# First token rows of an encoder layer: products of the identity on TensorE while they load, three row buffers of their own, and gate weights asked for behind the second and the fourth block

## The chip, the cores and the metric

The kernel runs on one core of one Trainium2 chip. The metric is the time of one execution in device microseconds (us), lower is better. The kernel before was timed three times: 1777.31, 1779.03 and 1780.24 us, median 1779.03.

## The reference

One layer of a streaming encoder, for 1024 prompt tokens and 64 sample tokens that share the weights (D = 1024, all float32):

```
h = rmsnorm(x, g_mix);  p = h @ w_in
qa, ka, va, qi, ki, wi, ub, qm, gates = split(p)
A: s = relu(qi . ki) per index head; score = sum_h s * wi; per query the top 256 (sample: 48)
   admissible keys by score; softmax attention over those
B: per channel group of 128: trailing mean over 2/4/8/16 frames minus the token, then a 128x128 map
M: cross-attention into 256 memory tokens
x = x + (sum over A, B, M of sigmoid(gate) * (branch @ w_o)) @ w_out
x = x + (silu(rmsnorm(x) @ w_gate) * (rmsnorm(x) @ w_up)) @ w_down
```

Keys, values and indexer keys of the new tokens are outputs too.

## The kernel before

The tokens lie in nine blocks of 128 rows, b = 0 to 8 (the last one, the sample, has 64). All of it runs on one core, each engine working through its own list of instructions in order. A scheduler writes those lists at build time: it plays the program through with durations of its own and appends, on each engine, what it believes ready first. So a change at the beginning can move instructions much later on. In-order lists make one instruction that waits hold up all that stand behind it on the same engine. Every DMA is issued from SyncE (SP), whose list is in order too.

Float32 products are made in three passes: each operand is split into a rounded part and a rest (`whi`/`wlo` for weights, `hh`/`hl` for the normalized, transposed tokens), and `matmul3` (L115 to L121, the products on L120) issues hi*hi, hi*lo and lo*hi.

The stages that the prediction speaks of, in program order:

- **First rows** (L242 to L259). For each block: load the rows (L247), square and sum them on ScalarE (L252), take the reciprocal root on GpSimd (L124, L125), scale them on VectorE (L255), transpose them on TensorE in eight 128x128 pieces into two PSUM tiles `mm` (L131), round each of these to `hh` on ScalarE (L133) and take the rest `hl` on VectorE (L86). Even blocks load into `raw`, the three general weight buffers, odd blocks into two buffers `xt`. Behind blocks 0 and 2 `fgate` asks for a block of gate weights: load to `fraw` (L110), round to `whi` on GpSimd (L96), rest `wlo` on VectorE (L86).
- **Gates** (`fsig`, L230; products `fl<-hh` and `fl<-hl` on L120). One gate block over all tokens is three chunks of 364, 362 and 362 columns with 24 products each. 16 gate blocks, 1152 products, are filler: they stand between the other stages wherever the scheduler had TensorE free.
- **Index stage** (L266 to L351). Index weights come through the `raw` buffers into `tmhi`/`tmlo` (`tm_weights`, L169, L96, L86; three pieces of 888, 888 and 592 columns); `idx_proj` makes 24 products of 296 columns per block; then scores of every query with every key (L333, L334, L338). Cached keys `ck` enter through L286 and L278/L279.
- **Search** (`select`, from L735). The top 256 are found by bisection over 31 bits on score tiles, for three blocks with ScalarE counting (L765, results compared by `hit_a`, L784) and four with VectorE counting (L768, `hit_v`). Both loops step together in VectorE's list.
- **Mixer** (branch B, L385 to L448), four channel groups one behind the other. Per group: 72 products, running sums on GpSimd (L431), then on VectorE `pw` (L433, L435, L434), ScalarE rounds it to `ph` (L440), VectorE takes the rest `pl`, and TensorE multiplies both by `pwh`, `pwl`. Then `fill_ob` (products `fl<-bh`) needs all four groups.
- Then query and key projections, attention, output projection, feed-forward.

```
for b in range(NB):
    t0, n = TS[b]
    xt = xp.tile([128, D], F32, name="xt", tag="xt", bufs=2) if b % 2 else raw_tile()
    SP.dma_start(xt[:n], xrows(b))
    ...
    A.activation(junk[:n], xt[:n], AF.Square, accum_out=ss[:n])
    rstd(r[:n], ss[:n], 1.0 / D)
    V.scalar_tensor_tensor(xt[:n], xt[:n], r[:n], gmix[:n], op0=OP.mult, op1=OP.mult)
    transpose_split(xt, n, hh[:, :, t0:t0 + n], hl[:, :, t0:t0 + n])
    if b in (0, 2):
        first.append(fgate(8 + len(first)))
```

Of the kernel before, what the change touches and what calls it, by code (L numbers as in the profile page):

```python
# [8 lines left out]
F32 = mybir.dt.float32  # L9
# [7 lines left out]
D = 1024  # L17
# [28 lines left out]
def encoder_step(ctx: ExitStack, tc: tile.TileContext, a: dict, o: list):  # L46
    nc = tc.nc
    V, A, G, PE, SP = nc.vector, nc.scalar, nc.gpsimd, nc.tensor, nc.sync
# [12 lines left out]
    ident_r = const.tile([128, 128], F32R, name="ident_r")  # L61
# [6 lines left out]
    def bcast_row(dst, src, off, n):  # L68
        SP.dma_start(dst, bass.AP(tensor=src.tensor, offset=src.offset + off, ap=[[0, 128], [1, n]]))
# [7 lines left out]
    def mm(dt=F32):  # L77
        return psum[0].tile([128, 512], dt, name="mm", tag="mm", bufs=n_mm[0])
# [44 lines left out]
    def rstd(r, ss, inv):  # L123
        G.tensor_scalar(r, ss, inv, EPS, op0=OP.mult, op1=OP.add)  # L124
        G.tensor_tensor(r, r, mhalf[:r.shape[0], :r.shape[1]], op=OP.pow)  # L125

    def transpose_split(src, n, hi, lo):
        for g in range(0, KT, 4):
            ps = mm()
            for k in range(4):  # L130
                PE.transpose(ps[:, k * 128:k * 128 + n], src[:n, (g + k) * 128:(g + k + 1) * 128], ident[:n, :n])  # L131
            pv = ps.rearrange("p (k t) -> p k t", t=128)[:, :, :n]
            A.copy(hi[:, g:g + 4], pv)  # L133
            lo_of(lo[:, g:g + 4], pv, hi[:, g:g + 4])
# [59 lines left out]
    def xrows(b):  # L194
        return a["x_prompt"][b * 128:(b + 1) * 128] if b < 8 else a["x_sample"]

    def raw_tile():
        return wp.tile([128, 1024], F32, name="raw", tag="raw", bufs=3)
# [26 lines left out]
    def fgate(f):  # L225
        return wblock(a["w_gates"][f], (KT, 128), fraw())
# [14 lines left out]
    ip = ip_c.__enter__()  # L241
    with tc.tile_pool(name="xphase", bufs=1) as xp:  # L242
        gmix = xp.tile([128, D], F32, name="gmix")
        for b in range(NB):
            t0, n = TS[b]
            xt = xp.tile([128, D], F32, name="xt", tag="xt", bufs=2) if b % 2 else raw_tile()
            SP.dma_start(xt[:n], xrows(b))  # L247
            if b == 0:
                bcast_row(gmix, a["g_mix"], 0, D)
            junk = xp.tile([128, D], F16, name="xjunk", tag="xjunk", bufs=1)  # L250
            ss = xp.tile([128, 1], F32, name="ss", tag="ss", bufs=3)
            A.activation(junk[:n], xt[:n], AF.Square, accum_out=ss[:n])  # L252
            r = xp.tile([128, 1], F32, name="rs", tag="rs", bufs=3)
            rstd(r[:n], ss[:n], 1.0 / D)
            V.scalar_tensor_tensor(xt[:n], xt[:n], r[:n], gmix[:n], op0=OP.mult, op1=OP.mult)  # L255
            transpose_split(xt, n, hh[:, :, t0:t0 + n], hl[:, :, t0:t0 + n])
            if b in (0, 2):
                first.append(fgate(8 + len(first)))

    gqm_c = col("gqm_c", a["g_qm"], 1)  # L260
# [92 lines left out]
    with tc.tile_pool(name="mem", bufs=1) as mp:  # L353
# [6 lines left out]
        for i in range(2):  # L360
            xt = raw_tile()
# [88 lines left out]
    with tc.tile_pool(name="qm", bufs=1) as tp:  # L450
        for half in range(2):
            w = tm_weights(tp, a["w_qm"][half], 256)
            for b in range(NB):
                t0, n = TS[b]
# [6 lines left out]
    with tc.tile_pool(name="qa", bufs=1) as qp:  # L461
# [18 lines left out]
        for half in range(2):  # L480
            w = tm_weights(qp, a["w_qa"][half], 256)
            for b in range(NB):
                t0, n = TS[b]
# [28 lines left out]
        for b in range(NB):  # L512
            t0, n = TS[b]
# [822 lines left out]
```

## Time and profile before

| | |
|---|---|
| median of three runs | 1779.03 us (1777.31 to 1780.24) |
| the profiled execution's own time | 1782.27 us |
| its span, first to last instruction | 1780.5 us |
| TensorE products busy | 1721.8 us (97% of the span), 11810 instructions |
| VectorE busy | 1127.0 us (63%) |
| ScalarE busy | 816.4 us (46%) |
| GpSimd busy | 403.3 us (23%) |
| mean granted TensorE clock | 0.991 |

Engines: PE is TensorE, DVE VectorE, ACT ScalarE, POOL GpSimd, SPq the DMA issues of SyncE. L12 is line 12 of the kernel. The granted clock is a share of full speed: 1.00 is 2.4 GHz, 0.50 is 1.2 GHz. Products overlap in the pipeline: what one costs in a run of them is the distance between two starts, not its own duration.

### The profile page before, as it was taken

To read this page: it belongs to the slowest core of one execution; us is meant where nothing else is said; L and a number is where in the kernel's file an instruction comes from. 1 tells how busy PE (TensorE), PEld (TensorE's weight loads), DVE (VectorE), ACT (ScalarE), POOL (GpSimd) and SP (SyncE) were. 2 spreads that over 40 slices of the span, in tenths; PEclk is the share of its full clock that TensorE was granted. 3 is DMA by queue.
4 is the path that set the end of the run, shared out by engine and by line. 5 is a ranking of instruction groups with operands and counts; after the bars stand their busy time and mean duration, and the time that the engine had idled before them with its cause. 6 is when DMAs were issued, how large, how long until landed. Compare 5 with 4: busy or idle time off the path is not lost.

```text
span 1780.5 us, 31511 instructions
## 1 busy us (share of the span) xinstructions
PE 1721.8 (97%) x11810; PEld 1672.4 (94%) x11810; DVE 1127.0 (63%) x2411; ACT 816.4 (46%) x1927; POOL 403.3 (23%) x444
## 2 busy tenths in 40 slices
PE   7999999999999998989899998999999999999999
PEld 6999999989999998877798997999999999999999
DVE  6567999998953345779783858645444444544443
ACT  5456677726523443579631444433333333433332
POOL 4111423343531223765203521100000000000000
PEclk9999999999999999999999998999999999999999
DMA  7122541134355236640454333222222221857562
GB/s 230 60 67 76 164 141 57 58 98 137 118 157 176 84 97 233 188 154 1 165 184 146 98 120 110 92 73 73 73 73 77 92 75 38 316 184 239 187 229 98
DMA packets 128582, 224.26 MB, mean 126 GB/s; under 512 B 23463, under 2 KB 86303, under 8 KB 128430
## 3 DMA queue, kind: packets, MB, share of 16 engines
q1 hardware_dynamic: 128430, 222.26, 38.5%
q8 instruction: 93, 1.52, 0.3%
q14 instruction: 59, 0.48, 0.1%
HBM read 167.84 MB, written 54.37 MB: 125 GB/s over the span
## 4 chain that ended last, share of the span: by engine, by line
PE 61%; DVE 6%; DMA 2%; issue 1%; POOL 1%; ACT 1%; SPq 0%; DVEq 0%; ACTq 0%; POOLq 0%
PE mm L1115 24%; PE mm L1263 14%; PE mm L120 11%; PE fl L120 7%; PE acc L921 1%; PE tr L891 1%; DVE lo L86 1%; PE mm L914 1%; DVE wlo L86 1%; DVE fr L1071 1%; DMA side_a<-gt 1%; DVE ws L1078 0%; PE mm L603 0%; DVE pr L895 0%; DVE pl L86 0%
## 5 line engine op out<-in xcount | busy, mean ns | idle before, releaser
L1115 PE MATMUL mm<-hi,whi 128*128 128x288 f32 (+1 forms) x1120 | 324.0, 289 | 9.4 <-ACT whi L1107 8.3
L1115 PE MATMUL mm<-hi,wlo 128*128 128x288 f32 (+1 forms) x1120 | 324.9, 291 | 0.0
L1115 PE MATMUL mm<-lo,whi 128*128 128x288 f32 (+1 forms) x1120 | 324.2, 290 | 0.0
L1115 PEld LDWEIGHTS mm<-hi,whi 128*128 128x128 f32 x1120 | 212.6, 190 | 10.1 <-ACT whi L1107 8.5
L1115 PEld LDWEIGHTS mm<-lo,whi 128*128 128x128 f32 x1120 | 212.5, 190 | 0.0
L1115 PEld LDWEIGHTS mm<-hi,wlo 128*128 128x128 f32 x1120 | 211.9, 189 | 0.2 <-DVE wlo L86 0.2
L120 PE MATMUL fl<-hl,whi 128*128 128x362 f32 (+1 forms) x576 | 190.5, 331 | 0.0
L120 PE MATMUL fl<-hh,whi 128*128 128x362 f32 (+1 forms) x576 | 189.9, 330 | 0.6 <-ACT hh L133 0.6
L120 PE MATMUL fl<-hh,wlo 128*128 128x362 f32 (+1 forms) x576 | 189.3, 329 | 0.0
L1263 PE MATMUL mm<-uh,wh 128*128 128x362 f32 (+1 forms) x512 | 167.4, 328 | 0.0
L1263 PE MATMUL mm<-ul,wh 128*128 128x362 f32 (+1 forms) x512 | 166.8, 326 | 0.0
L1263 PE MATMUL mm<-uh,wl 128*128 128x362 f32 (+1 forms) x512 | 166.0, 326 | 0.0
L86 DVE TENSOR_TENSOR wl<-raw,wh 128x1024 fp32r<-128x1024 f32 x64 | 78.4, 1225 | 126.1 <-ACT wh L94 125.8
L94 ACT CAST wh<-raw 128x1024 fp32r<-128x1024 f32 x64 | 67.3, 1051 | 148.9 <-PE mm L1263 137.5
L120 PE MATMUL mm<-tmhi,hh 128*128 128x256 f32 (+3 forms) x432 | 122.8, 289 | 0.5 <-POOL tmhi L96 0.5
L120 PE MATMUL mm<-tmlo,hh 128*128 128x256 f32 (+3 forms) x432 | 122.5, 286 | 0.3 <-DVE tmlo L86 0.3
L120 PE MATMUL mm<-tmhi,hl 128*128 128x256 f32 (+3 forms) x432 | 122.3, 285 | 0.0
L765 ACT ACTIVATE junk_a<-score,cand_a,sgn_a 128x512 f16<-128x512 f32 (+2 forms) x93 | 95.5, 1027 | 46.8 <-DVE cand_a L782 22.7
L86 DVE TENSOR_TENSOR wlo<-raw,whi 128x1024 fp32r<-128x1024 f32 (+1 forms) x75 | 76.1, 1027 | 55.0 <-ACT whi L1107 39.7
L120 PEld LDWEIGHTS fl<-hh,whi 128*128 128x128 f32 x576 | 108.3, 188 | 1.6 <-issue 1.0
L120 PEld LDWEIGHTS fl<-hl,whi 128*128 128x128 f32 x576 | 108.4, 188 | 0.6
L120 PEld LDWEIGHTS fl<-hh,wlo 128*128 128x128 f32 x576 | 108.5, 188 | 0.6
(386 smaller groups left out, 4538.5 us busy)
## 6 DMA issues: line engine op xcount, KB each, us to landing
raw<-in_w_down_dram SPq DMA_DIRECT2D x66, 512.0 KB, 3.7
raw<-in_w_up_dram SPq DMA_DIRECT2D x26, 512.0 KB, 3.7
fraw<-in_w_gates_dram SPq DMA_DIRECT2D x24, 512.0 KB, 4.0
fr<-in_w_gate_dram SPq DMA_DIRECT2D x22, 512.0 KB, 3.6
side<-side_a SPq DMA_DIRECT2D x8, 1088.0 KB, 6.0
raw<-in_w_out_dram SPq DMA_DIRECT2D x16, 512.0 KB, 3.7
uf<-u SPq DMA_DIRECT2D x44, 181.0 KB, 3.7
u<-tg SPq DMA_DIRECT2D x22, 288.0 KB, 2.1
```

The source lines that it names most:

```text
L86: V.tensor_tensor(lo, src, hi.bitcast(F32), op=OP.subtract)
L94: A.copy(hi, src)
L120: PE.matmul(ps, l, r, start=i == 0, stop=i == n - 1)
L765: A.activation(junk[:n, :nk], sc, AF.Sign, bias=bj, scale=1.0 if scale is None else scale[:n, j:j + 1], accum_out=sj)
L891: PE.matmul(lg[:n, i * 512:i * 512 + cn], qT[:, h, :n], kT[:, kv, s, k0 + c:k0 + c + cn], start=s == 0, stop=s == 1)
L914: PE.transpose(pt[:cn, i * n:(i + 1) * n], probs[i][:, c:c + cn], ident[:n, :n])
L921: PE.matmul(acc, vv, r, start=ji == 0 and i == 0, stop=ji == nj - 1 and i == 1)
L1071: V.scalar_tensor_tensor(hb[e][:, :n], ys[i][:, kk], gffn_c[:, kk:kk + 1], rb[:, :n], op0=OP.mult, op1=OP.mult)
L1115: PE.matmul(dst[i], l, r, start=start and j == 0, stop=stop and j == 11, skip_group_check=True)
L1263: PE.matmul(acc[f], l, r, start=kb == 0 and j == 0, stop=kb == NF - 1 and j == 2)
```

## The change

Three edits in the loop over the first rows, and nothing elsewhere:

1. Before the loop 40 products of the 128x128 identity with itself are issued, and 20 more behind each of the blocks 0 and 1. They write a PSUM tile `spin` out of the five `mm` buffers that nobody reads. They need only `ident_r`, which is made on the core.
2. All blocks load into `xt`, which has three buffers now, and none into `raw`.
3. Gate weights are asked for behind blocks 1 and 3 rather than 0 and 2.

```
+        spin = mm()
+
+
+        def turn_over(n):
+            for _ in range(n):
+                PE.matmul(spin[:, :128], ident_r, ident_r, start=True, stop=True)
+
+        turn_over(40)
         for b in range(NB):
             t0, n = TS[b]
-            xt = xp.tile([128, D], F32, name="xt", tag="xt", bufs=2) if b % 2 else raw_tile()
+            xt = xp.tile([128, D], F32, name="xt", tag="xt", bufs=3)
             SP.dma_start(xt[:n], xrows(b))
...
             transpose_split(xt, n, hh[:, :, t0:t0 + n], hl[:, :, t0:t0 + n])
-            if b in (0, 2):
+            if b < 2:
+                turn_over(20)
+            if b in (1, 3):
                 first.append(fgate(8 + len(first)))
```

Lines behind the edit are 8 to 10 higher in the changed kernel (L255 becomes L263, L433 becomes L443).

SyncE's list. Before, five blocks of rows can be asked for at once: rows 0, `gmix`, gate weights, rows 1, 2, 3, 4, then the small `gqm_c`, `gffn_c`, `spool_c`, `cosi`, `sini`, `gk`, `ck`, then rows 6, gate weights, rows 5, 8, 7, then the index weights. Now: rows 0, `gmix`, rows 1, gate weights, rows 2, the same small ones up to `gk`, then the three pieces of index weights, `ck`, gate weights, rows 3, two blocks of memory rows, rows 4, a block of memory weights, gate weights, rows 5 and 6; rows 7 and 8 stand behind the first stores of gate results. Rows 3 can be asked for when the transposes of block 0 have freed their buffer.

VectorE's list at its head, before, from the scaling of block 0 on (`raw` and `xt` are rows):

```order
L255 SCALAR_TENSOR_TENSOR raw<-raw,rs,gmix 128x1024
L86 TENSOR_TENSOR wlo<-fraw,whi 128x1024
L86 TENSOR_TENSOR hl<-mm,hh 128x4x128
L255 SCALAR_TENSOR_TENSOR xt<-xt,rs,gmix 128x1024
L86 TENSOR_TENSOR hl<-mm,hh 128x4x128
L255 SCALAR_TENSOR_TENSOR raw<-raw,rs,gmix 128x1024
L263 TENSOR_SCALAR spool_c<-spool_c 128x4
L255 SCALAR_TENSOR_TENSOR xt<-xt,rs,gmix 128x1024
L86 TENSOR_TENSOR hl<-mm,hh 128x4x128
L255 SCALAR_TENSOR_TENSOR raw<-raw,rs,gmix 128x1024
L86 TENSOR_TENSOR hl<-mm,hh 128x4x128
L279 TENSOR_TENSOR k_364<-ck,k_364 128x64
```

And now, from the same place:

```order
L263 SCALAR_TENSOR_TENSOR xt<-xt,rs,gmix 128x1024 x2
L86 TENSOR_TENSOR wlo<-fraw,whi 128x1024
L273 TENSOR_SCALAR spool_c<-spool_c 128x4
L263 SCALAR_TENSOR_TENSOR xt<-xt,rs,gmix 128x1024
L86 TENSOR_TENSOR tmlo<-raw,tmhi 128x888
L86 TENSOR_TENSOR hl<-mm,hh 128x4x128 x2
L86 TENSOR_TENSOR tmlo<-raw,tmhi 128x888
L289 TENSOR_TENSOR k_445<-ck,k_445 128x64
L86 TENSOR_TENSOR tmlo<-raw,tmhi 128x592
L86 TENSOR_TENSOR wlo<-fraw,whi 128x1024
L86 TENSOR_TENSOR hl<-mm,hh 128x4x128 x2
L263 SCALAR_TENSOR_TENSOR xt<-xt,rs,gmix 128x1024
```

The rests `hl` of block 0 stand now behind a piece of the index weights (`tmlo`), those of block 1 behind the rest of these, the cached keys and the second gate weights; those of block 2 follow only behind the scaling of block 3. On TensorE the transposes of block 3 likewise stand ahead of the run of products of the first chunk, which needs blocks 0 to 2; before, those of blocks 3 and 4 did.

TensorE's list around the first product of the index stage (`mm_370`), before, with the buffers' numbers; `fl_4292` is a gate block on the second chunk of columns, and the transposes are those of block 8:

```order
L131 MATMUL mm_319<-ident_69,raw_310 128x64 x4
L131 MATMUL mm_326<-ident_69,raw_310 128x64 x4
L282 MATMUL mm_367<-ident_r_74,k4_364 128x128
L120 MATMUL fl_4292<-hl_105,whi_138 128x362
L120 MATMUL fl_4292<-hh_104,wlo_139 128x362
L120 MATMUL fl_4292<-hh_104,whi_138 128x362
L120 MATMUL mm_370<-tmhi_347,hh_104 128x296
```

And now (the index stage begins with `mm_451`; `fl_4401` is the second chunk, `fl_4429` and `fl_4457` are the third):

```order
L131 MATMUL mm_400<-ident_69,xt_391 128x64 x4
L131 MATMUL mm_407<-ident_69,xt_391 128x64 x4
L292 MATMUL mm_448<-ident_r_74,k4_445 128x128
L120 MATMUL fl_4401<-hh_104,whi_294 128x362
L120 MATMUL fl_4401<-hl_105,whi_294 128x362
L120 MATMUL fl_4401<-hh_104,wlo_295 128x362
L120 MATMUL fl_4401<-hh_104,whi_294 128x362
L120 MATMUL fl_4401<-hl_105,whi_294 128x362
L120 MATMUL fl_4401<-hh_104,wlo_295 128x362
L120 MATMUL fl_4429<-hh_104,whi_242 128x362
L120 MATMUL fl_4457<-hh_104,whi_294 128x362
L120 MATMUL mm_451<-tmhi_428,hh_104 128x296
```

More of the filler stands ahead of the index stage: before its first product 98 gate products instead of 72, before its last score product 584 instead of 551. At the first `ph` product of the fourth mixer group both lists have the same products behind them, all 1152 gate products and the first 27 of `fill_ob` among them (the change has its 80 products of the identity besides).

VectorE's list at the fourth mixer group, before (`hit_a` compares a step of the search):

```order
L771 TENSOR_SCALAR score_95<-score_95,sgn_a 128x512
L768 TENSOR_SCALAR junk_v,ssum_v<-score_96,cand_v 128x640
L433 TENSOR_TENSOR pw<-pw,fix 128x16
L435 SCALAR_TENSOR_TENSOR pw<-pw,e 128x1087
L771 TENSOR_SCALAR score_97<-score_97,sgn_a 128x768
L768 TENSOR_SCALAR junk_v,ssum_v<-score_98,cand_v 128x896
L434 TENSOR_TENSOR pw<-pw,e 128x16
L784 TENSOR_TENSOR hit_a<-ssum_a,cuta_a 128x3
```

And now:

```order
L794 TENSOR_TENSOR hit_a<-ssum_a,cuta_a 128x3
L781 TENSOR_SCALAR score_99<-score_99,sgn_a 128x1024
L794 TENSOR_TENSOR hit_v<-ssum_v,cuta_v 128x4
L795 SCALAR_TENSOR_TENSOR tbit_a<-hit_a,tbit_a 128x3
L795 SCALAR_TENSOR_TENSOR tbit_v<-hit_v,tbit_v 128x4
L798 TENSOR_SCALAR tbit_a<-tbit_a 128x3
L792 TENSOR_SCALAR cand_v<-tbit_v 128x4
L799 TENSOR_SCALAR cand_a<-tbit_a 128x3
L803 TENSOR_SCALAR shi_a<-tbit_a 128x3
L778 TENSOR_SCALAR junk_v,ssum_v<-score_100,cand_v 64x192
L800 TENSOR_SCALAR cand_a<-cand_a 128x3
L443 TENSOR_TENSOR pw<-pw,fix 128x16
```

The fourth group's `pw` stands behind 31 steps of the search now, all there are; before it stood behind 30. From the key attention on (L861) the lists of all engines are the same.

## Rows read from the trace of the kernel before

**Rows 1.** Busy time by stretch, all engines (stretch, length, busy us of each, PEclk, DMA, GB/s)
```profile
0.00:40.00 40.00, 27.10 (x156) 24.88 (x157) 29.98 (x72) 21.56 (x41) 18.61 (x30) 1.00 0.74 229
172.00:352.00 180.00, 177.86 (x1133) 176.19 (x1132) 171.31 (x488) 127.17 (x266) 59.84 (x47) 1.00 0.34 106
```
**Rows 2.** Timeline of TensorE, first 35 us (start, us, line, out<-in, count, idle before)
```profile
7.90 1.97 PE L131 MATMUL mm<-ident,raw 128*128 128x128 f32 x8 [7.90 <-DVE raw L255]
...
21.30 0.64 PE L120 MATMUL fl<-hl,whi 128*128 128x364 f32 x1
...
29.11 0.33 PE L120 MATMUL fl<-hl,whi 128*128 128x364 f32 x1
29.28 0.33 PE L120 MATMUL fl<-hh,wlo 128*128 128x364 f32 x1
29.44 1.04 PE L131 MATMUL mm<-ident,xt 128*128 128x128 f32 x8
...
33.57 0.66 PE L131 MATMUL mm<-ident,xt 128*128 128x128 f32 x4 [1.45 <-DVE hl L86]
```
**Rows 3.** Timeline of the fourth mixer group, on VectorE and TensorE
```profile
352.67 0.17 DVE L433 TENSOR_TENSOR pw<-pw,fix 128x16 f32<-128x16 f32 x1
...
357.64 0.76 PE L120 MATMUL mm<-ph,pwh 128*128 128x364 f32 x3 [1.09 <-ACT ph L440]
...
359.99 0.67 PE L120 MATMUL mm<-pl,pwh 128*128 128x364 f32 x1 [1.59 <-DVE pl L86]
```
**Rows 4.** Timeline of SyncE: three issues of the first 15 us
```profile
2.58 0.73 SPq L247 DMA_DIRECT2D raw<-in_x_prompt_dram  x1
...
3.84 0.45 SPq L247 DMA_DIRECT2D raw<-in_x_prompt_dram  x1
...
14.02 0.43 SPq L286 DMA_DIRECT2D ck<-in_cache_idx_k_dram  x1
```
**Rows 5.** The same three issues in the DMA view (count, KB, us from issue to landing)
```profile
raw<-in_x_prompt_dram SPq DMA_DIRECT2D x1, 512.0 KB, 7.7
...
raw<-in_x_prompt_dram SPq DMA_DIRECT2D x1, 512.0 KB, 9.4
...
ck<-in_cache_idx_k_dram SPq DMA_DIRECT2D x1, 16.0 KB, 3.5
```
**Rows 6.** Timeline of the other engines, first 36 us
```profile
2.27 0.22 DVE L62 CAST ident_r<-ident 128x128 fp32r<-128x128 f32 x1
...
4.45 1.06 ACT L252 ACTIVATE xjunk<-raw 128x1024 f16<-128x1024 f32 x1 [2.45 <-DMA raw<-in_x_prompt_dram]
...
6.56 1.28 DVE L255 SCALAR_TENSOR_TENSOR raw<-raw,rs,gmix 128x1024 f32<-128x1024 f32 x1 [3.77 <-POOL rs L125]
...
21.68 1.21 DVE L86 TENSOR_TENSOR wlo<-fraw,whi 128x1024 fp32r<-128x1024 f32 x1
...
26.20 0.93 POOL L96 TENSOR_SCALAR tmhi<-raw 128x888 fp32r<-128x888 f32 x1
...
28.13 1.07 DVE L86 TENSOR_TENSOR tmlo<-raw,tmhi 128x888 fp32r<-128x888 f32 x1
...
32.84 3.06 DVE L86 TENSOR_TENSOR hl<-mm,hh 128x512 fp32r<-128x512 f32 x5
```
**Rows 7.** Two stretches at the low clock (stretch, length, TensorE busy, PEclk, DMA, GB/s)
```profile
360.00:366.40 6.40, 6.40 (x20) 0.50 0.20 77
1086.00:1090.00 4.00, 4.00 (x15) 0.50 0.00 0
```
**Rows 8.** Timeline of VectorE: two comparisons of the search, one step apart
```profile
333.24 0.16 DVE L784 TENSOR_TENSOR hit_a<-ssum_a,cuta_a 128x3 int32<-128x3 f32 x1 [0.41 <-ACT junk_a L765]
...
337.37 0.16 DVE L784 TENSOR_TENSOR hit_a<-ssum_a,cuta_a 128x3 int32<-128x3 f32 x1 [0.27 <-ACT junk_a L765]
```
**Rows 9.** Who TensorE waited for from 420 to 520 us (total, times, longest)
```profile
PE fl L120 <- DVE fpt L549: 3.1, 2, 1.8
```

## Prediction

> **What bounds the kernel now.** I read the busy times by stretch first. TensorE is the bound: it works 177.9 of the 180 us from 172 to 352 us, but only 27.1 of the first 40 [rows 1]. So the change, all of it at the beginning, can win at most the 12.9 us that are missing there, unless it moves something else. The second row of the group shows what that could be: from 172 to 352 us VectorE works 171.3 us as well. That is the stretch of the search, and a list as full as this one cannot catch up.
>
> The timeline of TensorE's first 35 us tells what the 12.9 us are [rows 2]. The first transposes start at 7.90, when block 0 has been loaded and scaled. Eight of them take 1.97 us at that time and 1.04 us at 29.44: the same instruction, twice as fast later. PEclk reads 1.00 in this stretch [rows 1], so the column does not show the low level here, the durations do. The first gate product of the long run, at 21.30, takes 0.64 us; those of 29.11 and 29.28 take 0.33 us and start 0.17 us apart. The run of filler thus starts at 21.30, at once near the upper level, with one later wait of 1.45 us (33.57).
>
> Then the fourth mixer group [rows 3]. Its scaling `pw` starts on VectorE at 352.67, TensorE waits 1.09 us for `ph` and 1.59 us for `pl`. Ahead of that place both lists hold the same TensorE products, the last gate product included, so there is no filler left to put in. What sets the time there is when VectorE's search has come so far. A delay of the search goes into the total, and a delay of TensorE that is no longer than it costs nothing beside.
>
> **The change part by part.** *The products.* `ident_r` is ready at 2.49 [rows 6]. The trace has no ordinary 128-column product of `ident_r`; the nearest rows are transposes of that size, at most 0.25 us each cold (1.97/8) and 0.13 warm (1.04/8). So 40 end between 2.5 + 5.2 = 7.7 and 2.5 + 10 = 12.5, and block 0, scaled at 7.84 [rows 6], is transposed late by 0 to 4.7 us. I count nothing: VectorE takes up block 0's transposes only at 17.6 (below), and up to that delay this covers it. The Trainium skill (TensorE: Matmul & The Clock Gate, Part 1) gives 107 ns from start to start for bf16 products of 128 columns while cold; by it, an estimate, 40 products end at 6.8, and rival C below would lose its price.
>
> *The buffers, the gate weights and the index weights.* With `raw` free, index weights are asked for behind the small transfers, and VectorE's list has them ahead of `hl` of block 0. When do they land? The fifth 512 KB block lands at 2.58 + 7.7 = 10.3, the seventh at 3.84 + 9.4 = 13.2; `ck`, the last of the seven small ones, at 14.02 + 3.5 = 17.5 [rows 4, 5]. So the small ones take 4.3 us behind the blocks, and a block 1.45. Now five blocks stand ahead and six small ones (`ck` follows): 10.3 + 4.3 + some 1.0 to 1.45, about 15.6 (bounds: 11.8, if the small ones cost nothing, and 18.9, if nothing moves up). Block 2, landed at 10.3, is scaled 2.1 us later (4.45 to 6.56) plus 1.28 [rows 6], at 13.8 behind `wlo`. So VectorE stands still from 13.8 to 16.5, when GpSimd has rounded the first piece (0.93 [rows 6]).
>
> From 16.5 VectorE's list runs, by the spacings of [rows 6]: `tmlo` 1.07 to 17.6; two `hl`, 0.61 each, to 18.8; `tmlo` to 19.9; keys and the last `tmlo` (592 columns, two thirds) 0.9 to 20.8; `wlo` 1.21 to 22.0; two `hl` to 23.3; scaling of block 3 1.28 to 24.55. Then TensorE transposes block 3. It has stood nearly still since about 15, so at the low level: 1.97, to 26.5; meanwhile `hl` of block 2 is done. The run of gate products starts at 26.5 rather than 21.30: **+5.2**. Block 4's transposes lie behind that start now, warm 1.04: **+1.0**. And the run starts cold. After a wait at 1086 TensorE stayed at 0.50 for 4.0 us of work, at 360 for 6.4 us [rows 7], which costs half of it, 2.0 or 3.2; now 0.3 is lost so (0.64 less 0.33 at 21.30). I take the lower, after the longer wait: **+1.7**. The wait of 1.45 stays: the three blocks 4 to 6 come in a row as three did before. Front: **+7.9**. Low bound: index weights in time (-2.7), no cold start (-0.9 for block 3, -1.7): 2.6. High bound: weights at 18.9 (+3.3), 3.2 for the clock (+1.2): 12.4. Rows 7 and 8 load late, but TensorE then has the second chunk to do.
>
> *The order behind it.* The last score product has 33 more gate products ahead of it (584, 551), 0.17 us each [rows 2]: **+5.6** on the start of the search. This work isn't added, only moved; but filler done early is missing later, and at the fourth mixer group all of it has been done in both.
>
> *The search.* VectorE passes 31 comparisons rather than 30 ahead of the fourth `pw`; one step takes 337.37 - 333.24 = 4.13 us [rows 8]: **+4.1**. The rest of its list between the first comparison and that place is the same work. Bounds: 0, if it only takes idle time (VectorE has 8.7 us in those 180), and 4.1.
>
> So the fourth `pw` comes 7.9 + 5.6 + 4.1 = 17.6 us later. TensorE itself, only 7.9 later, waits some 10 us there, falls to the low level as it does now, and comes out 17.6 late. Behind that place it has the same work in much the same order, and no cover. One wait could go there: 3.1 us for `fpt` [rows 9], as VectorE is then ahead by comparison; I take none of it, as the row doesn't say what VectorE waited for, and keep 3.1 for the range.
>
> The profiled execution took 1782.27 us, so 1799.9 for it; it lies 3.2 above the median of the runs, 1779.03. On the median: **1796.6**.
>
> **The rivals.** *A, the search has slack.* If VectorE makes up for its late start, TensorE's own lateness is all: 1779 + 7.9 = 1786.9. For it: those 8.7 us of idle time. Against: TensorE waits for this chain twice already [rows 3], and the idle time comes in small pieces at the ends of steps [rows 8].
>
> *B, the front gets faster.* Warm transposes, and index weights that are there when VectorE comes to them: the five blocks ahead of the run save 5 x (1.97 - 1.04) = 4.7, and if the later order costs nothing either, the time is 1774.3. It decides whether the run of gate products starts before 21.3. For it: the two transpose rows of [rows 2]. Against: even with no wait for the index weights VectorE's list has 8.0 us of work from 13.8 to the end of block 3's scaling, and block 3's transposes take 1.04 more, so that the run starts at 22.9 or later. The Trainium skill (same page, Part 4) says that a transpose does not count as TensorE activity and that the upper level is not reached in transposes. The row at 29.44 contradicts the second half. By the rule rival B would be worth nothing; its chance here goes by VectorE's list alone.
>
> *C, the products don't do what they are for.* If they never raise the clock, 80 of them take up to 80 x 0.25 = 20 us; with four blocks' transposes at 1.97 TensorE is through with block 3 at 2.5 + 20 + 7.9 = 30.4: up to 3.9 later than in the forecast, 1796.6 to 1800.5.
>
> **How the numbers follow.** Forecast 0.70, A 0.15, C 0.09, B 0.06. The forecast's own bounds: 2.6 + 5.6 + 0 - 3.1 = 5.1 gives 1784; 12.4 + 5.6 + 4.1 = 22.1 gives 1801. C ends at 1800, A's middle lies at 1787. The range 1783 to 1802 holds these and leaves out B and what is stranger, under 2 in 10. A measurement of this kernel tells about 0.2%, 3.6 us, from no change. Faster: B, 0.06. The same: A with the low front (2.6), and a little of the forecast's low end: 0.06. Slower: the rest, 0.88.
>
> **What would show it.** In the changed profile: the identity products from 2.5 us, the transposes of blocks 0 and 1 near 1.04 per eight; a wait of VectorE for `tmhi` between 14 and 16.5, with `hl` of block 0 behind it; the gate run from about 26.5; the first comparison of the search some 13 us later than now; a wait of TensorE of about 10 us ahead of the fourth `ph`; after that everything later by 17.6 us. Wrong would be: a gate run that begins before 22; a fourth `ph` without a long wait; or a PE idle total that does not grow by about what the time does.

## The result and the profile after

The changed kernel takes 1795.18 us (median of 6 runs, 1790.53 to 1797.74), the kernel before, beside it, 1779.63 (1777.05 to 1784.46). The ratio is 1.0085, with a 95% interval of 1.0067 to 1.0103: slower by about 15 us. Forecast were 1796.6 and a range of 1783 to 1802.

The profiled execution took 1793.94 us, its span is 1791.9. The busy times of the two stretches of [rows 1] in the changed kernel (stretch, length, busy us of TensorE, its weight loads, VectorE, ScalarE, GpSimd, then PEclk, DMA, GB/s):

```profile
0.00:40.00 40.00, 33.94 (x187) 33.10 (x188) 24.84 (x64) 17.26 (x32) 15.26 (x26) 0.96 0.80 247
172.00:352.00 180.00, 177.09 (x1124) 174.31 (x1123) 167.32 (x471) 126.14 (x268) 47.57 (x43) 1.00 0.35 108
```

TensorE is busier in the first 40 us than before (27.10), and has done less in them: part of the 33.94 are the products of the identity. The timeline of TensorE's first 31 us, beside [rows 2]:

```profile
2.55 8.80 PE L249 MATMUL mm<-ident_r 128*128 128x128 f32 x40 [2.55 <-DVE ident_r L62]
11.15 1.93 PE L131 MATMUL mm<-ident,xt 128*128 128x128 f32 x8
12.73 4.51 PE L249 MATMUL mm<-ident_r 128*128 128x128 f32 x20
17.04 1.93 PE L131 MATMUL mm<-ident,xt 128*128 128x128 f32 x8
18.62 2.84 PE L249 MATMUL mm<-ident_r 128*128 128x128 f32 x20
21.29 1.06 PE L131 MATMUL mm<-ident,xt 128*128 128x128 f32 x8
...
26.32 1.94 PE L131 MATMUL mm<-ident,xt 128*128 128x128 f32 x8 [2.95 <-DVE xt L263]
27.92 0.65 PE L120 MATMUL fl<-hl,whi 128*128 128x364 f32 x1
...
29.81 0.33 PE L120 MATMUL fl<-hl,whi 128*128 128x364 f32 x1
```

TensorE is not idle from 2.55 to 22.3, and all the same only the third batch of products runs faster (20 in 2.7 us; the second 20 in 4.3). The transposes of blocks 0 and 1 take 1.93, as cold as before. Then TensorE waits 2.95 us for block 3's scaling and has lost the clock: the next eight transposes take 1.94, and the run of gate products begins at 27.92, cold, instead of 21.30.

What it waited for, in VectorE's and GpSimd's timeline (beside [rows 6]):

```profile
13.89 1.29 DVE L263 SCALAR_TENSOR_TENSOR xt<-xt,rs,gmix 128x1024 f32<-128x1024 f32 x1 [0.64 <-POOL rs L125]
17.54 1.08 DVE L86 TENSOR_TENSOR tmlo<-raw,tmhi 128x888 fp32r<-128x888 f32 x1 [2.36 <-POOL tmhi L96]
18.54 1.28 DVE L86 TENSOR_TENSOR hl<-mm,hh 128x512 fp32r<-128x512 f32 x2
...
23.71 1.28 DVE L86 TENSOR_TENSOR hl<-mm,hh 128x512 fp32r<-128x512 f32 x2
24.91 1.27 DVE L263 SCALAR_TENSOR_TENSOR xt<-xt,rs,gmix 128x1024 f32<-128x1024 f32 x1
...
16.57 3.49 POOL L96 TENSOR_SCALAR tmhi<-raw 128x888 fp32r<-128x888 f32 x3 [2.71 <-DMA raw<-in_w_idx_dram]
...
22.78 1.41 POOL L125 TENSOR_TENSOR rs<-rs,mhalf 128x1 f32<-128x1 f32 x1
```

The index weights land at 16.57 us and VectorE stands before `tmlo` for them, with the rests `hl` of block 0 behind it, those of block 1 and the scaling of block 3 behind the remaining pieces. VectorE's list is not the only thing that is late there. Rows 3, asked for at 14.21 behind the index weights, land at 21.03, and GpSimd has block 3's root only at 24.19, 0.7 us before VectorE comes to the scaling at 24.91:

```profile
21.03 1.06 ACT L260 ACTIVATE xjunk<-xt 128x1024 f16<-128x1024 f32 x1 [1.31 <-DMA xt<-in_x_prompt_dram]
```

Now the places where the lateness can be read: the last score product, the first comparison of the search, the fourth `pw`, the fourth `ph` product, and the first product of the query stage far behind. The kernel before (the fourth group stands in [rows 3]):

```profile
170.40 0.34 PE L333 MATMUL mm<-kstack,qt 128*64 128x192 f32 x2
173.19 0.30 DVE L784 TENSOR_TENSOR hit_a<-ssum_a,cuta_a 128x3 int32<-128x3 f32 x1
567.93 0.38 PE L623 MATMUL mm<-ident,qn 128*128 128x128 f32 x2
```

The changed kernel:

```profile
182.68 0.25 PE L343 MATMUL mm<-kstack,qt 128*64 128x192 f32 x1
185.33 0.16 DVE L794 TENSOR_TENSOR hit_a<-ssum_a,cuta_a 128x3 int32<-128x3 f32 x1 [0.34 <-ACT junk_a L775]
372.30 0.16 DVE L443 TENSOR_TENSOR pw<-pw,fix 128x16 f32<-128x16 f32 x1
375.48 1.27 PE L120 MATMUL mm<-ph,pwh 128*128 128x364 f32 x3 [11.26 <-ACT ph L450]
582.47 0.38 PE L633 MATMUL mm<-ident,qn 128*128 128x128 f32 x2
```

The scores end 12.3 us later, of which 33 x 0.17 = 5.6 is gate products that now stand ahead of them; the other 6.7 is lateness. TensorE comes to the fourth `ph` at 375.48 - 11.26 = 364.22, before at 357.64 - 1.09 = 356.55: still 7.7 late. There it waits 11.26 us instead of 1.09. The `ph` product is 17.8 later than before, the query stage 14.5. From the key attention on the lists are the same; there this execution made up another 2.8 us (TensorE idle for 13.8 us in that stage, 16.3 before; the kernels of the experiments have 14.0 to 18.0 there), so the spans differ by 11.4, while the medians differ by 15.6.

### The profile page after: what moved, and what is told of

Read it like the earlier page. It is cut to its first block, busy times and chain, and to the rows that moved or that the text cites. A ratio compares the mean times of both kernels' runs of the same rounds, so it can differ in the third digit from the quotient of the medians.

```text
span 1791.9 us, 31671 instructions
## 1 busy us (share of the span) xinstructions
PE 1733.7 (97%) x11890; PEld 1684.1 (94%) x11890; DVE 1125.6 (63%) x2411; ACT 817.8 (46%) x1927; POOL 397.2 (22%) x444
## 4 chain that ended last, share of the span: by engine, by line
PE 48%; DVE 4%; ACT 1%; issue 1%; POOL 1%; DMA 0%; DVEq 0%; POOLq 0%; ACTq 0%
PE mm L1125 24%; PE mm L1273 14%; PE mm L120 7%; DVE lo L86 1%; PE acc L931 1%; DVE fr L1081 1%; PE tr L901 1%; PE mm L924 0%; DVE ws L1088 0%; DVE wlo L86 0%; POOL ws L1088 0%; DMA fr<-in_w_gate_dram 0%; ACT pr L907 0%; ACT ph L927 0%; DVE pl L86 0%
```

## The experiments

All runs were timed against the kernel before on the same chip; its medians there were 1778.71 us (for runs 1, 2, 4 and 5), 1778.33 (3 and 6 to 8) and 1779.39 (9 to 12). "Lateness" in what follows is the start of the last score product against 170.40, less 0.17 us for each gate product that was moved ahead of it.

### 1 to 3: the edits one by one

*Gate weights alone* (behind blocks 1 and 3, the kernel before otherwise):

```
-            if b in (0, 2):
+            if b in (1, 3):
```

> The kernel before, with the gate weights asked for behind blocks 1 and 3 as the only edit. Two theories of what the changed order costs. Search theory (the prediction's terms): the start of the search and the number of comparisons ahead of the fourth pw set the time of the fourth mixer group. Here 549 gate products stand ahead of the last score product (551 before) and 30 comparisons ahead of the fourth pw (30 before), so the time stays: 1779.6 us, within 1.5. Filler theory: what counts is how many gate products stand ahead of the fourth group's own 72 products, because from their end to the fourth ph runs a chain of some 19 us (copies, running sums, pw, ph) that only the gate products left over can cover. Here 1078 stand ahead of them instead of 1048: 30 x 0.166 = 5.0 us later, some of it given back behind, so 1783 to 1785, and a wait of TensorE of about 6 us ahead of the fourth ph.

Measured: 1778.84 us, ratio 1.0005 (0.9992 to 1.0018). The time stays. The last score product starts at 170.43 and the first comparison at 173.82. The filler theory had its chain right and the end wrong:

```profile
354.59 0.43 PE L120 MATMUL fl<-bh,whi 128*128 128x362 f32 x1 [1.24 <-ACT fsg L235]
...
359.22 0.43 PE L120 MATMUL fl<-bh,whi 128*128 128x362 f32 x1 [2.88 <-ACT fsg L235]
...
361.59 0.77 PE L120 MATMUL mm<-ph,pwh 128*128 128x364 f32 x3 [0.63 <-ACT ph L440]
```

The fourth `ph` does come 4.0 us later (361.59 against 357.64), about the 5.0 that 30 gate products ahead of it take. TensorE waits 4.75 us in all up to there, in three pieces (1.24, 2.88, 0.63), against 1.3 before (0.2, 1.09); the theory said about 6. The search theory's "the time stays" came true, but not by its terms: `ph` moved by 4.0 us where the first comparison moved by 0.6. At the query stage this kernel is 2.0 us ahead of the kernel before (565.94 against 567.93; 8 gate products, 1.3 us, are done later there). Of these 6 us, 3.1 are the waits for `fpt` [rows 9], which are gone; where the rest came back was not resolved. So neither a `ph` that is 4 us late nor some 4 us of idle TensorE ahead of it are a loss by themselves.

*Products alone* (the 40 + 20 + 20 products of the identity in the kernel before):

```
+        turn_over(40)
...
+            if b < 2:
+                turn_over(20)
```

> The kernel before, with the 80 products of the identity as the only edit. Front: at 0.22 us each (as in the changed kernel) they push the five blocks' transposes back, the run of gate products starts near 24 instead of 21.3: +3. The order of the rest is that of the run with the gate weights alone (549 gate products ahead of the last score product, 30 comparisons ahead of the fourth pw, 1078 gate products ahead of the fourth group's own). Search theory: front alone, 1782 to 1783. Filler theory: 3 + 5.0, less some that is given back, 1786 to 1788.

Measured: 1785.22 us, ratio 1.0041 (1.0027 to 1.0055), 6.5 us. The front behaves as expected: the run begins near 24 (its first product at 23.32), lateness 2.9 + 2 x 0.17 = 3.2. The total lost twice that, above the search theory's figure and just below the filler theory's. Against the run before, with the same lists behind the front, 1.9 us of it are a wait for `tmlo` behind the fourth group that was not there; which of the later waits belong to the delay and which to chance stays open.

*Buffers alone* (three for all rows, the kernel before otherwise):

```
-            xt = xp.tile([128, D], F32, name="xt", tag="xt", bufs=2) if b % 2 else raw_tile()
+            xt = xp.tile([128, D], F32, name="xt", tag="xt", bufs=3)
```

> The kernel before with the three row buffers as the only edit (gate weights behind blocks 0 and 2, no products). Its lists from the index stage on are the changed kernel's (584 gate products ahead of the last score product, 1116 ahead of the fourth group's own). If the buffers alone, by the earlier index weights, make the later order and its wait, the time is that of the changed kernel without products, 1790 to 1793, with a wait of some 11 us ahead of the fourth ph. If the gate weights had a part in it, it is 1786 or less.

Measured: 1794.12 us, ratio 1.0086 (1.0071 to 1.0101). The buffers alone cost as much as the whole change. Lateness 3.4 us (score product at 179.41), and ahead of the fourth `ph` the changed kernel's wait:

```profile
371.10 1.27 PE L120 MATMUL mm<-ph,pwh 128*128 128x364 f32 x3 [11.25 <-ACT ph L440]
```

### 4: the changed kernel without the products

```
-        turn_over(40)
...
-            if b < 2:
-                turn_over(20)
```

> The changed kernel without its 80 products of the identity; three row buffers and gate weights behind blocks 1 and 3 stay. The order from the index stage on is the changed kernel's (584, 31, 1116), and on TensorE three blocks rather than four are transposed ahead of the run of gate products. Search and filler theory agree: what the order costs stays, the front loses its lateness, as the run can start near 18 (but cold, and with block 3 and 4 behind it): lateness ahead of the fourth group 0 +- 3 us instead of 7.7, total 1785 to 1790. If the products had helped the front (by the clock), it is 1795 or more.

Measured: 1791.74 us, ratio 1.0076 (1.0060 to 1.0092): 13.0 of the loss remain. The score product starts at 177.62, lateness 1.6 instead of 6.7, so the products cost the front 5.1 us, and the wait is there unchanged (TensorE, fourth `ph`):

```profile
370.47 1.27 PE L120 MATMUL mm<-ph,pwh 128*128 128x364 f32 x3 [11.26 <-ACT ph L440]
```

VectorE's timeline shows why the products cost so much:

```profile
11.86 0.68 DVE L86 TENSOR_TENSOR hl<-mm,hh 128x512 fp32r<-128x512 f32 x1
...
13.59 0.68 DVE L86 TENSOR_TENSOR hl<-mm,hh 128x512 fp32r<-128x512 f32 x1
...
15.46 1.27 DVE L86 TENSOR_TENSOR hl<-mm,hh 128x512 fp32r<-128x512 f32 x2
17.19 1.08 DVE L86 TENSOR_TENSOR tmlo<-raw,tmhi 128x888 fp32r<-128x888 f32 x1 [0.46 <-POOL tmhi L96]
```

Without them the rests of blocks 0 and 1 are through by 16.7, ahead of the first `tmlo`. With them the blocks are transposed at 11.15 and 17.04, and the scheduler, which plays the products through as well, puts the index weights first.

### 5: one gate block held back

```
+    with tc.issue_after(u_at.ins):
+        fill_gate(16, side_m[:, 0], 7, 8)
```

(`u_at` is the last of all 72 of the fourth group's own products, not of the first chunk's, as the expectation has it: in the trace they end at 353.49, and the 72 held gate products begin at 353.65; `issue_after` queues what it encloses behind it on the same engine.)

> The changed kernel, with the last of the 16 gate blocks (72 products) queued on TensorE behind the first chunk of the fourth mixer group's own products. By the lists this moves 36 gate products from ahead of that group's products to behind them (1080 ahead instead of 1116) and leaves everything else as it is: 31 comparisons ahead of the fourth pw, 584 gate products ahead of the last score product. Search theory: the fourth ph comes when it came, the time stays at 1795. Filler theory: the group's products, and with them the fourth ph, come 36 x 0.166 = 6.0 us earlier, TensorE's wait of 11.3 falls to about 5, total 1788 to 1791.

Measured: 1798.47 us, ratio 1.0114 (1.0095 to 1.0132): not faster, if anything slower. The wait ahead of the fourth `ph` falls to 1.69, and TensorE waits 6.97 us one group earlier, where it waited 0.99:

```profile
338.37 1.27 PE L120 MATMUL mm<-ph,pwh 128*128 128x364 f32 x3 [6.97 <-ACT ph L451]
...
372.44 0.76 PE L120 MATMUL mm<-ph,pwh 128*128 128x364 f32 x3 [1.69 <-ACT ph L451]
```

TensorE was there in time, and the third `ph` came only 1.4 us earlier (338.37 against 339.77), 1.1 of which the first group had already (276.81 against 277.94). The groups' pace is not set by the filler between them; how that filler is dealt out decides only ahead of which group TensorE stands. What the filler ahead of the first group does, this run leaves as it was.

### 6 to 8: the fourth `pw` earlier in VectorE's list

In the first attempts one count of the search was queued behind the fourth `pw` (in the third attempt one count in each group):

```
-                    V.tensor_scalar(junk[:n, :nk], sc, bj, None, op0=OP.is_ge, op1=OP.add, accum_out=sj)
+                    behind = PIN.get((bit, j))
+                    with nullcontext() if behind is None else tc.issue_after(pw_last[behind].ins):
+                        V.tensor_scalar(junk[:n, :nk], sc, bj, None, op0=OP.is_ge, op1=OP.add, accum_out=sj)
```

> The changed kernel, with one count of the search (640 columns, 29th step of the tiles that VectorE counts) queued on VectorE behind the scaling pw of the fourth mixer group. Nothing else moves: pw stands a few counts earlier in VectorE's list, TensorE's list is the same. In the changed kernel's trace the running sums that pw needs end at 366.8 and pw starts at 372.3. Search theory: VectorE's list sets pw, ph and TensorE's wait, so pw starts near 367, the wait of 11.3 falls to 6, and 5 us come off the total: 1789 to 1791. Rival (the wait is only the place where an earlier loss shows, and what is saved there is waited for behind): pw comes 5 earlier, but the total stays within 1.5 of 1795.

> The same in the kernel before: the 896-column count of the 28th step is queued behind the fourth pw. There pw starts at 352.7, the running sums end at 347.7, and TensorE waits 1.09 and 1.59 us and then works 6.4 us at the low clock. Search theory: pw at 348.7, both waits go, 2.7 us off, and up to 3.2 more if the clock stays up: 1773 to 1776. Rival (saved there, waited for behind): 1778.7 within 1.5.

> As before_pin4, with the pw of the other three groups brought forward too, by 1.4, 1.9 and 3.7 us of VectorE's counts. TensorE waits 1.8 us for ph ahead of the third group and earlier. Search theory: 1 to 2 us more than before_pin4, 1771 to 1775. Rival: no better than the kernel before, as TensorE has work enough up to the fourth group.

Measured: 1796.94 us for the changed kernel (ratio 1.0108, 1.0092 to 1.0123), and for the kernel before 1779.65 with one `pw` (1.0000, 0.9989 to 1.0011) and 1781.37 with all four (1.0011, 0.9996 to 1.0026). The first does not test what it was meant to: the scheduler filled the place with the search's other branch, and `pw` came later, not earlier (372.30 in the changed kernel):

```profile
373.21 0.17 DVE L444 TENSOR_TENSOR pw<-pw,fix 128x16 f32<-128x16 f32 x1
...
378.33 1.27 PE L120 MATMUL mm<-ph,pwh 128*128 128x364 f32 x3 [13.87 <-ACT ph L451]
```

In the kernel before the fourth `pw` did not come the 4 us earlier that were meant, but 0.8 later (353.48) and, with all four, 1.4 earlier (351.31), so these two do not test it either; what they show is that the time does not follow such small shifts.

### 9: the same, with everything in between moved

Two counts, the last comparison `hit_a` and the tail of the search's first branch are queued behind the fourth `pw` of the changed kernel:

```
+            with tc.issue_after(pw_last[3].ins) if on_act and bit == 0 else nullcontext():
                 V.tensor_tensor(hit, ssum, cuta, op=OP.is_ge)
...
+              with tc.issue_after(pw_last[3].ins):
                 V.tensor_scalar(snk[:, j:j + 1], cuta[:, j:j + 1], 0.5, (1 + nk) / 2.0, op0=OP.mult, op1=OP.add)
                 signed(b, n, j)
```

> The changed kernel with what stood on VectorE between the end of the running sums (366.8) and the fourth pw (372.3) queued behind that pw: two counts of the 29th step, the last comparison hit_a and the search's tail. One rest wlo stays ahead. Search theory: pw at about 368, ph and TensorE's products 4 us earlier, 3 to 4 us off the total: 1791 to 1793. Rival (what is saved there is waited for behind, as VectorE has the counts still to do): pw comes earlier, the total stays within 1.5 of 1795.

Measured: 1791.06 us, ratio 1.0073 (1.0060 to 1.0086), against 1.0085 of the changed kernel. VectorE and TensorE:

```profile
366.09 0.16 DVE L444 TENSOR_TENSOR pw<-pw,fix 128x16 f32<-128x16 f32 x1
...
368.80 1.28 PE L120 MATMUL mm<-ph,pwh 128*128 128x364 f32 x3 [6.29 <-ACT ph L451]
```

`pw` comes 6.2 us earlier (1.7 of it because this execution ran the group that much earlier as a whole: its running sums begin at 355.31 instead of 357.03), the wait falls from 11.26 to 6.29, and the total by 2 to 4 us, as the search theory said; the intervals of the two ratios still overlap. The order of VectorE's list is the last link of the wait: the running sums end at 365.08 here and `pw` follows 1.0 us later, against 5.5 in the changed kernel (and 5.0 in the kernel before). Some 6 us of the wait are left with nothing of the search in between, so they lie further back, in the lateness with which the group began.

### 10 and 11: index weights asked for behind the rows

```
             SP.dma_start(xt[:n], xrows(b))
+            if b == 6:
+                row_ld = ld
...
-        w = tm_weights(ip, a["w_idx"], 296)
+        with tc.issue_after(row_ld.ins):
+            w = tm_weights(ip, a["w_idx"], 296)
```

> The changed kernel, all three edits kept, with the three loads of index weights queued on SyncE behind the rows of block 6. VectorE's list then has no tmlo ahead of the rests hl of blocks 0 to 2. By the lists 566 gate products stand ahead of the last score product (before 551, changed 584), 30 steps ahead of the fourth pw (30, 31), 1074 gate products ahead of the fourth group's own (1048, 1116). If the index weights' place is what costs (prediction): the front is late by about 3 us as with the products alone, the order adds 15 x 0.17 = 2.5, TensorE's wait ahead of the fourth ph falls from 11.3 to 3 or less, total 1783 to 1787. If it is the late rows (three buffers instead of five), which this edit keeps: 1793 or more.

> The same without the products of the identity. If the index weights' place costs and the products cost some 3 us more: 1779 to 1783, no wait of over 3 us ahead of the fourth ph. If the late rows cost: as the changed kernel without products, 1791 or more.

Measured: 1789.21 us with the products (ratio 1.0063, 1.0049 to 1.0076), 1785.54 without (1.0040, 1.0025 to 1.0054). Between the two expectations, nearer to the first: about 6 us of the changed kernel's loss go, and about 7 of that without products. The long wait is gone in both, with waits for `fsg` of 4.9 and 5.5 us in all as what is left ahead of the fourth `ph`; TensorE of the first:

```profile
363.63 0.50 PE L120 MATMUL fl<-bh,whi 128*128 128x362 f32 x1 [3.74 <-ACT fsg L235]
...
370.30 0.77 PE L120 MATMUL mm<-ph,pwh 128*128 128x364 f32 x3 [0.79 <-ACT ph L453]
```

What did not go is the front. With products the gate run now begins at 22.80, but the score product starts at 180.54, lateness 10.1 - 15 x 0.17 = 7.6; without them 2.7. So the index weights' place costs by the order behind the front, not by the front: in TensorE's timeline 810 gate products stand ahead of the first mixer group in both, 848 in the changed kernel, and 38 x 0.166 = 6.3 us is about what the time gave back.

### 12: one buffer more

```
-            xt = xp.tile([128, D], F32, name="xt", tag="xt", bufs=2) if b % 2 else raw_tile()
+            xt = xp.tile([128, D], F32, name="xt", tag="xt", bufs=3) if b % 2 else raw_tile()
```

> The kernel before with a third buffer xt beside the three of raw, six for the rows in all, and nothing else. The rows of block 5 can be asked for earlier. The wait of 1.45 us at 33.57 may go, the order is 549, 30, 1078. Theory: what sets the first 21 us is the chain of load, squares, root and scaling of the first blocks, which this leaves: 1777 to 1780, no change. Rival (buffers bound the front): up to 3 us faster, 1775 to 1777.

Measured: 1779.01 us, ratio 0.9996 (0.9982 to 1.0010). The scores end 2.9 us earlier than before (167.54) and the total does not move. A front of 3 us either way is thus not simply 3 us of the time. No version beat the kernel before.

### The edits side by side

| kernel | lateness at the last score product | gate products ahead of the first group (793 before) | first / fourth `ph` product later by | wait ahead of the fourth `ph` | ratio to before |
|---|---|---|---|---|---|
| gate weights alone | 0.4 | 814 | 3.6 / 4.0 | 0.63 | 1.0005 |
| products alone | 3.2 | 814 | 6.5 / 6.9 | 0.63 | 1.0041 |
| buffers alone | 3.4 | 848 | 13.4 / 13.5 | 11.25 | 1.0086 |
| buffers and gate weights | 1.6 | 848 | 12.8 / 12.8 | 11.26 | 1.0076 |
| all three (the change) | 6.7 | 848 | 17.9 / 17.8 | 11.26 | 1.0085 |
| all, index weights late | 7.6 | 810 | 10.8 / 12.7 | 0.79 | 1.0063 |
| buffers and gate weights, index weights late | 2.7 | 810 | 6.9 / 9.0 | none | 1.0040 |

The wait column has only the wait for `ph` itself. Where it is short, waits for `fsg` stand shortly before it: 4.1 us with either the gate weights or the products alone, 4.9 and 5.5 in the last two rows.

## Why the prediction was right, and where it was not

**The place and most of the mechanism** hold: late by the front, later still by the order, no filler left at the fourth mixer group, and TensorE idle there. Forecast were "some 10 us" of waiting; 11.26 were measured, 10.2 more than before. Runs 3 and 4 show that this wait belongs to the buffers. That TensorE is idle there because of VectorE's search does not hold (see the search, below).

**Front, +7.9:** 6.7 at the last score product, 7.7 at the fourth group. Step by step it went as read: index weights at 16.57 (forecast 15.6), first `hl` at 18.5 (17.6), scaling of block 3 at 24.9 (forecast 23.3 to 24.55 for it), cold transposes, gate run at 27.92 (26.5). One thing the forecast has no term for: rows 3 themselves came late, so that block 3 could not have been scaled before 24.19 by any order of VectorE's list.

**The products, counted at nothing: wrong.** "VectorE takes up block 0's transposes only at 17.6, and up to that delay this covers it" is true in the list of the change, but that list was made with the products in it. Taken away they give 5.1 us of lateness back; alone they cost 6.5 us of time. The cover was made by the thing that it covered. Their size lay in the bounds: 40 end 8.8 us after 2.55, 0.22 each. The Trainium skill's 107 ns from start to start for bf16 products of 128 columns while cold (TensorE: Matmul & The Clock Gate, Part 1) isn't what these fp32r products do; the sum by bounds was the better one. The forecast marker that the transposes of blocks 0 and 1 would take 1.04 is refuted by 1.93: rival C's slow products came largely true, but of its extra 3.9 us only 1.4 (27.92 against 26.5), part of which is the index weights' later landing.

**The order, +5.6** on the start of the search: the first comparison is 12.1 later, 5.4 more than the lateness. Right.

**The search, +4.1: the step that failed.** "What sets the time there is when VectorE's search has come so far": it is not. The fourth `pw` is 19.6 later, the search's last comparison only 14.1 (370.56 against 356.44, 30 steps behind the first in both). As late as `pw`, within 0.5 us, are the running sums that it needs, and the group's own products on TensorE. First the kernel before (TensorE, TensorE, TensorE, GpSimd), then the changed one (the same, and VectorE's last comparison):

```profile
236.01 0.33 PE L120 MATMUL mm<-hh,uhi 128*128 128x364 f32 x1
260.05 0.67 PE L120 MATMUL mm<-ph,pwh 128*128 128x364 f32 x3
320.91 0.33 PE L120 MATMUL mm<-hh,uhi 128*128 128x364 f32 x1
337.87 2.05 POOL L431 TENSOR_TENSOR pw<-e 128x1117 f32<-128x1117 f32 x1 [18.03 <-DVE tbit_v L785]
```

```profile
253.06 0.33 PE L120 MATMUL mm<-hh,uhi 128*128 128x364 f32 x1
277.94 0.67 PE L120 MATMUL mm<-ph,pwh 128*128 128x364 f32 x3
340.37 0.33 PE L120 MATMUL mm<-hh,uhi 128*128 128x364 f32 x1
357.03 2.05 POOL L441 TENSOR_TENSOR pw<-e 128x1117 f32<-128x1117 f32 x1 [18.84 <-DVE tbit_v L795]
370.56 0.15 DVE L794 TENSOR_TENSOR hit_a<-ssum_a,cuta_a 128x3 int32<-128x3 f32 x1
```

(The sum reads `e`, whose last copy ScalarE ends at 356.89, 0.06 before the `tbit_v` that the row names.) The fourth group's own products begin 19.5 later, the sums 19.2, and `pw` follows the end of the sums by 5.5 us, by 5.0 before. Nor did the lateness arise there: the first group's `ph` product is 17.9 later already, the fourth's 17.8. The four groups are a chain, as each group's own products stand on TensorE right behind the first `ph` product of the group before (320.31 and 320.91, 339.77 and 340.37), and from the first `ph` to the fourth it takes 97.6 us before and 97.5 now. The search has its part in that pace, but the same part in both.

What is late is the chain's beginning, 17.05 us. TensorE waits only 0.4 us between 40 and 320 us before, and 1.9 between 40 and 339 now, so its list decides: 55 more gate products stand ahead of the first group (848, 793), 55 x 0.166 = 9.1, on top of a front of 6.7 to 7.7. Run 1 tests this alone: 21 more gate products (3.5 us), no lateness, and a first `ph` 3.6 later (263.68). So the forecast's 5.6 + 4.1 = 9.7 for order and search stands where 9.1 of moved filler belongs; that the two are near each other is luck.

The 4.13 us for a step [rows 8] was mis-sized besides: that step has nothing of the mixer beside it. Over the 30 steps from 173.19 to 356.44 one takes 6.1 on the mean, and one of them, on VectorE in the kernel before, 8.3:

```profile
341.49 0.58 DVE L784 TENSOR_TENSOR hit_a<-ssum_a,cuta_a 128x3 int32<-128x3 f32 x1 [0.27 <-ACT junk_a L765]
...
349.78 0.15 DVE L784 TENSOR_TENSOR hit_a<-ssum_a,cuta_a 128x3 int32<-128x3 f32 x1
```

**What was given back.** "I take none of it" of the 3.1 us for `fpt` [rows 9]: 2.3 went, 0.8 is left in the changed kernel. From `pw` to the first `ph` product it took 3.2 us instead of 5.0, so `ph` is 17.8 late where `pw` is 19.6. 17.8 - 2.3 = 15.5 is still 1 us more than the 14.5 at the query stage; that I cannot place.

**The rivals.** A (slack in the search, 1786.9) would want no long wait, and there is one. B (faster front) fails at its own condition, a gate run before 21.3. Of the filler theory, which came up behind the result, this much stands: gate products done early are what TensorE lacks later, and those ahead of the first group set when the groups' chain begins. That the place of the filler between the groups sets the time is refuted by run 5 (the wait moves a group ahead), and run 1 lost 4 us at the fourth `ph` without losing time.

**Open:** gate weights alone and products alone have the same lists behind the front and are 2.9 us apart at the fourth `ph` (361.59, 364.49), but 6.4 us apart in time; no run separates the waits behind it that add the rest. How much of a late fourth `ph` is given back behind it differs from kernel to kernel in the same way (the table). For run 12 part of the answer stands in its list: 814 gate products ahead of the first group instead of 793, so that its first `ph` comes 0.8 us later than before (260.84) in spite of the front that it gains.

## What to carry to other kernels

Work that fills an idle engine is free only if nothing else is decided by when it ends: here a scheduler moved other instructions because of it, so "the wait beside it covers it" has to be read from the list without the filler as well. Freeing a buffer lets somebody else in first: look who asks for it next, and what his arrival puts ahead of the work that was to be sped up. And where several things are late at one place, look which of them was late first: here the groups had been late by the whole amount from the first one on.

## What the runs showed of the hardware that was not expected

**Products of the identity do not raise the clock soon.** TensorE issued them without a gap from 2.55 us (with sixteen transposes between), and only at about 19.6, inside the third batch, did their spacing fall from 0.22 us to 0.11 (in run 10, 12 of them from 19.77 to 21.11). In the kernel without them, the gate products that began at 21.30 were at the upper level by 24.2. So 17 us of products brought the upper level 4.6 us earlier than no products with these buffers; in the kernel before, with transposes and two gate products from 12.69 on and no products of the identity, the gate product at 21.75 already takes 0.36. And behind the wait of 2.95 us the level was lost again. The PEclk column reads 1.00 for 2 to 22 us, and 0.50 for 27 to 29; in the first stretch only the durations tell the clock.

**VectorE's smallest instructions stretch beside GpSimd's running sums.** Four columns of integers take 0.17 us, and 1.99 when a sum starts. VectorE, then GpSimd, of the changed kernel:

```profile
356.99 0.17 DVE L792 TENSOR_SCALAR cand_v<-tbit_v 128x4 int32<-128x4 int32 x1
...
362.26 1.99 DVE L792 TENSOR_SCALAR cand_v<-tbit_v 128x4 int32<-128x4 int32 x1
...
362.19 4.63 POOL L441 TENSOR_TENSOR pw<-pw 128x1111 f32<-128x1111 f32 x2
```

The Trainium skill (GPSIMD Engine Reference, 8. Key points) says that GpSimd shares its SBUF interfaces with VectorE and that the two contend when a VectorE instruction is in a 2-port mode or has two SBUF inputs; the rows agree that they contend. That the stretched instruction has one input is what the row shows; in which mode it ran, no run here shows. It is part of why a step of the search takes 8.3 us beside a group's sums and 4.1 without.
